# Down projection of a decoder block's FFN: nine of its 22 pairs of channel tiles as two-by-two block products with seven multiplications instead of eight

## The chip, the cores and the metric

One core of a Trainium2 chip runs the whole kernel. The metric is the device time of one execution in microseconds (us), the median over the runs shown; lower is better.

## The reference

A decoder block: RWKV-7 time mixing and a forgetting attention run side by side over 272 positions (16 meta tokens and 256 tokens), are gated and merged, pass `w_o`, and are added to the residual `h`. Then comes the feed-forward part, which is where the change lies. All is float32.

```python
gate, up = jnp.split(_rms(h, n2) @ w_gu, 2, axis=-1)
return h + (jax.nn.silu(gate) * up) @ w_dn
```

Here `w_gu` is 2048 x 11264 and `w_dn` 5632 x 2048; the last product, the down projection, takes the activation `a` = silu(gate) * up, 256 tokens x 5632 channels, to 256 x 2048.

## The kernel before, in words

**Products in three parts.** A float32 operand is split in two fp32r parts, a high one (a copy, made by ScalarE) and a low one (operand minus high, made by VectorE). A product is three matmuls into the same PSUM bank: high by high, low by high, high by low. Each weight tile of 128 x 1024 numbers (512 KB) is loaded by a DMA issued on SyncE into a buffer `raw` (four of them, `RAWB`), then split into `wh` (ScalarE, L324) and `wl` (VectorE, L325), of which there are four each (`WB`). All this is in `wload`.

**Jobs.** The work is a list of jobs. A job has a `load` (the DMA and the split) and a `mul` (the matmuls); `run` calls the load of a job and then the `mul` of the one before, so that loads are written one job ahead. Only TensorE keeps the order in which it is written (`manual_schedule`). For ScalarE, VectorE, GpSimd and SyncE the framework's scheduler lays the instructions of the whole program into one fixed row per engine, by data that it expects to be ready and free buffers; on the chip each engine takes its row strictly in order and waits on semaphores. `slot` counts the time of the matmuls written so far and lets generators that were handed to `spawn` write their next step when it is due.

**Gate and up.** Eleven blocks of 512 channels; `post_up` (L1382 to L1388) multiplies, and `split`s the activation into `ach` and `acl` (128 channels x 44 channel tiles x 256 tokens, high and low). `ga` is a group of eight buffers of 128 x 256 for the gates, `ub` two such buffers.

**Down projection (L1391 to L1403).** Four blocks `j` of 512 output columns. In each, `tm_jobs` (L1297) runs over 22 pairs of channel tiles: a job loads two tiles of 128 channels x 512 columns and makes 12 matmuls: two channel tiles by two token tiles by three parts. `dn` is the accumulator, one PSUM bank for each token tile. The activation is the stationary operand (128 x 128), the weight the moving one (512 columns). After pair 22, `post` adds the bank to the residual in `hh` on VectorE (L1400) and writes it out; the last block does so in halves, one of them on ScalarE's queue.

PSUM has eight banks: four `main` (used by `dn`) and four `aux`.

The few lines of the loop on TensorE:

```python
for k, t in ((0, 0), (1, 0), (0, 1), (1, 1)):
    ...
    nc.tensor.matmul(o, ah[:, kt, ts_], hi, start=first, stop=False)
    nc.tensor.matmul(o, al[:, kt, ts_], hi, start=False, stop=False)
    nc.tensor.matmul(o, ah[:, kt, ts_], lo_, start=False, stop=last)
```

## Time and profile before

| | us |
|---|---|
| median of 3 runs | 1526.89 (1526.59 to 1528.88) |
| the profiled execution's own time | 1526.46 |
| its span, first to last instruction | 1524.8 |
| down projection on TensorE, first to last matmul | 1278.0 to 1520.6 |

The granted TensorE clock is 1.00 over the run. Times inside the execution count from the start of the span. In the profile PE is TensorE's matmuls, PEld its weight loads, DVE VectorE, ACT ScalarE, POOL GpSimd, SP SyncE. The columns of a group are busy us and mean ns of one instruction, then the idle time ahead of it on its engine and what ended it.

### The profile page before, as it was taken

Reading aid. Unit: us, or ns where it says so; the run is one execution under the profiler, and the core shown is the slowest. Engines: PE = TensorE matmul, PEld = TensorE weight load, DVE = VectorE, ACT = ScalarE, POOL = GpSimd, SP = SyncE. Lnnn points to the kernel's source line nnn. Section 1 sums busy time; section 2 is a strip of 40 time slices with the busy share of each in tenths; the row PEclk is TensorE's granted clock in tenths of the full one; section 3 lists DMA queues with packets and bytes.
Section 4 is the critical chain, followed back from the end, with each engine's and each line's share of the span. In section 5 each row is a group of like instructions: output and inputs, shape, how many; then the busy total and the mean of one; then the engine's idle time right before and its main releaser. Section 6 shows DMA issues by size and latency. Waiting matters only on the chain.

```text
span 1524.8 us, 25932 instructions
## 1 busy us (share of the span) xinstructions
PE 1518.6 (100%) x10113; PEld 1347.6 (88%) x10113; DVE 1028.4 (67%) x1853; ACT 781.1 (51%) x1184; POOL 103.1 (7%) x182
## 2 busy tenths in 40 slices
PE   9999999999999999999999999999999999999999
PEld 9999999989989888998888888888888888888887
DVE  8888699699689758776565566656556665444443
ACT  7754665564475545554455455545545554333332
POOL 2121203302202100000000000000000000000000
PEclk9999999999999999999999999999999999999999
DMA  8567456646645847767566666666666666666663
GB/s 273 164 178 200 130 143 187 179 116 178 187 125 156 224 143 224 234 221 246 181 180 182 192 192 186 192 190 192 186 191 191 190 191 188 191 205 205 191 204 105
DMA packets 211931, 283.30 MB, mean 186 GB/s; under 512 B 24096, under 2 KB 129072, under 8 KB 211808
## 3 DMA queue, kind: packets, MB, share of 16 engines
q1 hardware_dynamic: 206912, 277.25, 61.9%
q10 hardware_dynamic: 4896, 4.40, 0.8%
q8 instruction: 79, 1.29, 0.3%
q14 instruction: 44, 0.36, 0.1%
HBM read 274.36 MB, written 7.24 MB: 185 GB/s over the span
## 4 chain that ended last, share of the span: by engine, by line
PE 98%; ACT 1%; DVE 0%; DMA 0%; issue 0%; SPq 0%; DVEq 0%; ACTq 0%
PE up L430 11%; PE gt L430 10%; PE zg L430 8%; PE dn L1317 5%; PE dn L1319 5%; PE dn L1318 5%; PE up L432 5%; PE gt L432 5%; PE zg L432 4%; PE f L354 2%; PE f L356 2%; PE f L355 2%; PE br L354 2%; PE br L355 2%; PE br L356 2%; PE wo L1317 2%
## 5 line engine op out<-in xcount | busy, mean ns | idle before, releaser
L325 DVE TENSOR_TENSOR wl<-raw,wh 128x1024 fp32r<-128x1024 f32 x488 | 597.8, 1226 | 409.5 <-ACT wh L324 406.5
L324 ACT ACTIVATE wh<-raw 128x1024 fp32r<-128x1024 f32 x488 | 516.8, 1060 | 597.9 <-PE dn L1318 140.0
L430 PE MATMUL gt<-hts,wh 128*128 128x512 f32 x704 | 242.9, 392 | 0.0
L430 PE MATMUL up<-hts,wh 128*128 128x512 f32 x704 | 242.7, 392 | 0.0
L432 PE MATMUL gt<-hts,wl 128*128 128x256 f32 x660 | 184.8, 280 | 0.0
L432 PE MATMUL up<-hts,wl 128*128 128x256 f32 x660 | 184.5, 280 | 0.0
L430 PE MATMUL zg<-xhl,wh 128*128 128x512 f32 x512 | 181.2, 399 | 0.0
L430 PEld LDWEIGHTS up<-hts,wh 128*128 128x128 f32 x704 | 129.9, 188 | 25.2
L430 PEld LDWEIGHTS gt<-hts,wh 128*128 128x128 f32 x704 | 129.9, 188 | 25.1
L1317 PE MATMUL dn<-wh,ach 128*128 128x512 f32 x352 | 138.3, 393 | 0.0
L1319 PE MATMUL dn<-wl,ach 128*128 128x512 f32 x352 | 138.1, 392 | 0.0
L1318 PE MATMUL dn<-wh,acl 128*128 128x512 f32 x352 | 137.7, 391 | 0.0
L432 PE MATMUL zg<-xhl,wl 128*128 128x256 f32 x480 | 134.3, 280 | 0.0
L432 PEld LDWEIGHTS up<-hts,wl 128*128 128x128 f32 x660 | 125.3, 190 | 1.8
L432 PEld LDWEIGHTS gt<-hts,wl 128*128 128x128 f32 x660 | 125.3, 190 | 1.8
L430 PEld LDWEIGHTS zg<-xhl,wh 128*128 128x128 f32 x512 | 94.3, 188 | 18.7 <-issue 0.7
L432 PEld LDWEIGHTS zg<-xhl,wl 128*128 128x128 f32 x480 | 91.0, 190 | 1.2
L1319 PEld LDWEIGHTS dn<-wl,ach 128*128 128x128 f32 x352 | 66.0, 187 | 15.3
L1318 PEld LDWEIGHTS dn<-wh,acl 128*128 128x128 f32 x352 | 66.1, 188 | 14.9
L1317 PEld LDWEIGHTS dn<-wh,ach 128*128 128x128 f32 x352 | 66.1, 188 | 14.6
L354 PE MATMUL f<-xhl,wh 128*128 128x272 f32 x256 | 76.3, 298 | 0.0
L356 PE MATMUL f<-xhl,wl 128*128 128x272 f32 x256 | 73.7, 288 | 0.0
(463 smaller groups left out, 2789.6 us busy)
## 6 DMA issues: line engine op xcount, KB each, us to landing
raw<-in_w_gate_up_dram SPq DMA_DIRECT2D x176, 512.0 KB, 4.3
raw<-in_w_in_dram SPq DMA_DIRECT2D x160, 512.0 KB, 3.8
raw<-in_w_down_dram SPq DMA_DIRECT2D x88, 512.0 KB, 4.6
raw<-in_w_o_dram SPq DMA_DIRECT2D x32, 512.0 KB, 3.9
raw<-in_w_branch_a_dram SPq DMA_DIRECT2D x16, 512.0 KB, 4.4
raw<-in_w_branch_b_dram SPq DMA_DIRECT2D x16, 512.0 KB, 3.8
zgd<-zg ACTq DMA_DIRECT2D x30, 128.0 KB, 3.8
gate<-zgd SPq DMA_DIRECT2D x15, 256.0 KB, 5.5
```

The lines of the kernel that those rows point to most:

```text
L324: nc.scalar.activation(th, rr, AF.Copy)
L325: nc.vector.tensor_tensor(tl, rr, th.bitcast(F32), op=ALU.subtract)
L354: nc.tensor.matmul(ps, wh, ah, start=first, stop=False)
L355: nc.tensor.matmul(ps, wh, al, start=False, stop=False)
L356: nc.tensor.matmul(ps, wl, ah, start=False, stop=last)
L430: nc.tensor.matmul(ps.rearrange("p (a t) -> p a t", a=2), wh, act, start=first, stop=last)
L432: nc.tensor.matmul(ps[:, :T], wl, act[:, 0, :], start=False, stop=False)
L1317: nc.tensor.matmul(o, ah[:, kt, ts_], hi, start=first, stop=False)
L1318: nc.tensor.matmul(o, al[:, kt, ts_], hi, start=False, stop=False)
L1319: nc.tensor.matmul(o, ah[:, kt, ts_], lo_, start=False, stop=last)
```

## The change

**Layout.** The output columns are taken in two halves of 1024 (`cg`), not in four blocks. For a pair of channel tiles and a half, the weight is a block matrix of two channel tiles by two column blocks, b11, b12, b21, b22, and the activation one of two token tiles by two channel tiles, a11, a12, a21, a22. Four accumulators `cs` (`dn00` to `dn03`: c11, c12, c21, c22) take the four `main` banks.

**Slow pairs** (13 of 22) are as before: eight products of three matmuls, in two jobs of one column block each (`slow_jobs`).

**Fast pairs** (4 to 12, `FAST`) use seven products (`fast_jobs`), in the Winograd form of Strassen's scheme. With S1 = a21+a22, S2 = S1-a11, S3 = a11-a21, S4 = a12-S2 and T1 = b12-b11, T2 = b22-T1, T3 = b22-b12, T4 = b21-T2, the products are: a11 b11, S1 T1, S2 T2, S3 T3, each into a bank of its own (`dnp`: the four `aux` banks, summed over all fast pairs); S4 b22 into c12, a12 b21 into c11, a22 T4 into c21. After the last fast pair of a half, `sums_of_products` (L1546 to L1548) adds the four banks into the residual `hh`: one ScalarE copy and eight VectorE additions of 128 x 512.

**Loads of a fast pair.** Two `raw` buffers (`ra`: b11, b12; `rb`: b22, b21), filled by one DMA of 512 KB and two of 256 KB. Four jobs: b11 is split (half a tile), then b22 and b21, then T1 to T4 are made by four VectorE subtractions of 128 x 512 (L1510) into two buffers `tt`, and split as two tiles.

**Sums of the activation** (`sums_of_pairs`). S1 to S4 for all nine fast pairs are made once, in five batches (two pairs each, the last one): ten GpSimd operations of 128 x 256 (L1427; 128 x 128 in the last) into four `ga` buffers, then four ScalarE copies (L1440) and four VectorE subtractions (L1441) split them into `sst` (S1 to S3), and S4 into the place of a21 in `ach`/`acl`. The batches' buffers are `s2`, `s4`, `s6`, `s8`, `s9` with the number of the sum behind (`s60` is the first of the third batch). The third batch takes over the buffers of the first, the fourth those of the second, the second those of the last gates (`ga100` to `ga103`).

**Order.** First half: slow pairs 0 to 3, then nine times a fast and a slow pair. Second half: slow pair 0, nine times a fast and a slow pair, three slow pairs.

On each engine the program's rows stand as follows; numbers behind names tell buffers apart. First ScalarE at the start of the down projection, before. `wh_14431`, `wh_14449`, `wh_14467` are the weights of jobs 3, 4 and 5 (counted from 0).

```order
L324 ACTIVATE wh_14431<-raw_14430 128x4x256
L436 ACTIVATE ub102_14360<-up10_2_14174 128x256
L436 ACTIVATE ub103_14367<-up10_3_14175 128x256
L324 ACTIVATE wh_14449<-raw_14448 128x4x256
L499 ACTIVATE ach_9874<-ub102_14360 128x256
L499 ACTIVATE ach_9874<-ub103_14367 128x256
L324 ACTIVATE wh_14467<-raw_14466 128x4x256
L324 ACTIVATE wh_14485<-raw_14484 128x4x256
L324 ACTIVATE wh_14503<-raw_14502 128x4x256
L324 ACTIVATE wh_14521<-raw_14520 128x4x256
```

The same place after; `wh_14488` and `wh_14506` are jobs 5 and 6.

```order
L1440 ACTIVATE sst_14324<-s42_14448 128x2x128
L1440 ACTIVATE ach_9874<-s43_14449 128x2x128
L332 ACTIVATE wh_14488<-raw_14487 128x4x256
L507 ACTIVATE ach_9874<-ub102_14375 128x256
L507 ACTIVATE ach_9874<-ub103_14382 128x256
L1440 ACTIVATE sst_14324<-s60_14525 128x2x128
L1440 ACTIVATE sst_14324<-s61_14526 128x2x128
L1440 ACTIVATE ach_9874<-s63_14528 128x2x128
L1440 ACTIVATE sst_14324<-s62_14527 128x2x128
L332 ACTIVATE wh_14506<-raw_14505 128x4x256
L332 ACTIVATE wh_14546<-raw_14545 128x4x256
```

Between the weight copies now stand the copies of the sums: job 5's copy stands behind all four copies of the second batch, and job 6's behind all four of the third; each of these waits for GpSimd.

Next VectorE a little later, before: the last split of the activation, and splits of weights.

```order
L500 TENSOR_TENSOR acl_9875<-ub102_14360,ach_9874 128x256
L500 TENSOR_TENSOR acl_9875<-ub103_14367,ach_9874 128x256
L325 TENSOR_TENSOR wl_14468<-raw_14466,wh_14467 128x4x256
L325 TENSOR_TENSOR wl_14486<-raw_14484,wh_14485 128x4x256
L325 TENSOR_TENSOR wl_14504<-raw_14502,wh_14503 128x4x256
```

The same engine after, at the first fast pair. `wl_14596` and `wl_14598` are the splits of T1, T2 and of T3, T4; `raw_14673` and `raw_14674` are `ra` and `rb` of the next fast pair.

```order
L508 TENSOR_TENSOR wl_14585<-raw_14564,wh_14584 128x4x256
L1441 TENSOR_TENSOR sst_14324<-s81_14622,sst_14324 128x2x128
L1441 TENSOR_TENSOR sst_14324<-s82_14623,sst_14324 128x2x128
L1441 TENSOR_TENSOR acl_9875<-s83_14624,ach_9874 128x2x128
L1441 TENSOR_TENSOR sst_14324<-s90_14709,sst_14324 128x128
L1441 TENSOR_TENSOR sst_14324<-s91_14710,sst_14324 128x128
L508 TENSOR_TENSOR wl_14596<-tt_14599,wh_14595 128x4x256
L1441 TENSOR_TENSOR sst_14324<-s92_14711,sst_14324 128x128
L1510 TENSOR_TENSOR tt_14727<-raw_14673 128x512
L1441 TENSOR_TENSOR acl_9875<-s93_14712,ach_9874 128x128
L1510 TENSOR_TENSOR tt_14727<-raw_14674,tt_14727 128x512
L508 TENSOR_TENSOR wl_14598<-tt_14600,wh_14597 128x4x256
```

The splits of the fourth and fifth batch's sums (L1441) stand ahead of both weight splits of the first fast pair, and the next pair's first subtraction (from `raw_14673`) stands ahead of the current pair's last split. The second of these repeats: T1 of the next pair stands ahead of the last split in eight of the first half's fast pairs, and in four later pairs of the second half.

Last VectorE where one block of columns ends and the next begins, before.

```order
L325 TENSOR_TENSOR wl_14756<-raw_14754,wh_14755 128x4x256
L325 TENSOR_TENSOR wl_14778<-raw_14776,wh_14777 128x4x256
L325 TENSOR_TENSOR wl_14798<-raw_14796,wh_14797 128x4x256
L1400 TENSOR_TENSOR hh_9122<-dn0_0_14380,hh_9122 128x512
L1400 TENSOR_TENSOR hh_9122<-dn0_1_14381,hh_9122 128x512
L325 TENSOR_TENSOR wl_14816<-raw_14814,wh_14815 128x4x256
```

The same engine after, where the first half ends: `wl_15322` is the last split of pair 12, `wl_15347` and `wl_15369` the two jobs of the last slow pair, `wl_15391` the first job of the second half.

```order
L508 TENSOR_TENSOR wl_15322<-tt_15324,wh_15321 128x4x256
L333 TENSOR_TENSOR wl_15347<-raw_15345,wh_15346 128x4x256
L1548 TENSOR_TENSOR hh_9122<-dnp00_14588,hh_9122 128x512
L1548 TENSOR_TENSOR u0_15357<-dnp02_14590,u0_15357 128x512
L1548 TENSOR_TENSOR hh_9122<-dnp01_14589,hh_9122 128x512 x2
L1548 TENSOR_TENSOR hh_9122<-u0_15357,hh_9122 128x512
L333 TENSOR_TENSOR wl_15369<-raw_15367,wh_15368 128x4x256
L1548 TENSOR_TENSOR u0_15357<-dnp03_14591,u0_15357 128x512
L1556 TENSOR_TENSOR hh_9122<-dn00_14395,hh_9122 128x512
L1548 TENSOR_TENSOR hh_9122<-u0_15357,hh_9122 128x512 x2
L1556 TENSOR_TENSOR hh_9122<-dn02_14397,hh_9122 128x512
L333 TENSOR_TENSOR wl_15391<-raw_15389,wh_15390 128x4x256
```

The additions of the products' banks (L1548) and of the accumulators (L1556) stand between the splits of the jobs that TensorE takes next.

The diff, without its blank lines (of the functions above all is shown):

```diff
--- before.py
+++ after.py
@@ -63,6 +63,14 @@
 LANES = 108
 BETWEEN = 2
 MIX = 0.47
+FAST = [4, 5, 6, 7, 8, 9, 10, 11, 12]
+BATCHES = (2, 2, 2, 2, 1)
+SLOW = [0, 1, 2, 3] + list(range(13, 22))
+ORDER = [SLOW[:4] + [i for pair in zip(FAST, SLOW[4:]) for i in pair],
+         SLOW[:1] + [i for pair in zip(FAST, SLOW[1:10]) for i in pair] + SLOW[10:]]
+PAIRS = 8000
 HOP = 3050
 PREP = 5200
@@ -1388,18 +1396,174 @@
                 split(ach[:, 4 * j + m, :], acl[:, 4 * j + m, :], ub)
         run(cm_jobs(wgu[:, j * 512:(j + 1) * 512], KT, hts, NMETA, T, post_gate, name=f"gt{j}"))
         run(cm_jobs(wgu[:, DFF + j * 512:DFF + (j + 1) * 512], KT, hts, NMETA, T, post_up, alloc=aux_ps, name=f"up{j}"))
     wdn = A["w_down"][0]
-    for j in range(4):
-        js = slice(j * 512, (j + 1) * 512)
-        def post(t, ps, j=j):
-            n = 256 if j == 3 else 512
-            for c in range(512 // n):
-                cs_ = slice(j * 512 + c * n, j * 512 + (c + 1) * n)
-                nc.vector.tensor_tensor(hh[:, t, cs_], ps[:, c * n:(c + 1) * n], hh[:, t, cs_], op=ALU.add)
-                (nc.scalar if c else nc.sync).dma_start(out[0][t * P:(t + 1) * P, cs_], hh[:, t, cs_])
-        run(tm_jobs(wdn[:, js], NF, ach, acl, post, f"dn{j}"))
+    fast = FAST
+    slow = [i for i in range(NF // 2) if i not in fast]
+    acp_h, acp_l = (t.rearrange("p (i k) (t c) -> p i k t c", k=2, t=2) for t in (ach, acl))
+    sst = hp.tile([P, KT, 2, L], F32R, tag="hts", name="sst").rearrange("p k a t -> p (k a t)")
+    sst = sst[:, :len(fast) * 6 * P].rearrange("p (i s a c) -> p i s a c", i=len(fast), s=3, a=2)
+    def sums_of_pairs():
+        at = 0
+        for n in BATCHES:
+            fs, ps_ = slice(at, at + n), slice(fast[at], fast[at] + n)
+            at += n
+            h = lambda k, t: acp_h[:, ps_, k, t, :].bitcast(F32)
+            l = lambda k, t: acp_l[:, ps_, k, t, :].bitcast(F32)
+            f = [sst[:, fs, i, 1, :] for i in range(3)] + [acp_l[:, ps_, 0, 1, :]]
+            hi = [sst[:, fs, i, 0, :] for i in range(3)] + [acp_h[:, ps_, 0, 1, :]]
+            f32 = [hp.tile([P, T], F32, tag="ga", name=f"s{at}{i}", bufs=8)[:, :n * P].rearrange("p (i c) -> p i c", c=P)
+                   for i in range(4)]
+            def tt(i, x_, y_, op):
+                nc.gpsimd.tensor_tensor(f32[i], x_, y_, op=op)
+            tt(0, h(0, 1), h(1, 1), ALU.add)
+            tt(0, f32[0], l(0, 1), ALU.add)
+            tt(0, f32[0], l(1, 1), ALU.add)
+            tt(1, f32[0], h(0, 0), ALU.subtract)
+            tt(1, f32[1], l(0, 0), ALU.subtract)
+            tt(2, h(0, 0), h(0, 1), ALU.subtract)
+            tt(2, f32[2], l(0, 0), ALU.add)
+            tt(2, f32[2], l(0, 1), ALU.subtract)
+            tt(3, h(1, 0), f32[1], ALU.subtract)
+            tt(3, f32[3], l(1, 0), ALU.add)
+            yield PAIRS
+            for i in range(4):
+                nc.scalar.activation(hi[i], f32[i], AF.Copy)
+                nc.vector.tensor_tensor(f[i], f32[i], hi[i].bitcast(F32), op=ALU.subtract)
+    def a_of(i, k, t):
+        return acp_h[:, i, k, t, :], acp_l[:, i, k, t, :]
+    def s_of(i, n):
+        return a_of(i, 0, 1) if n == 3 else tuple(sst[:, fast.index(i), n, a, :] for a in range(2))
+    def rows(ap):
+        return ap.rearrange("p (r c) -> p r c", c=T)
+    def product(ps, a, w, half, first, last):
+        o = ps.rearrange("p (a c) -> p a c", a=2)
+        hi, lo_ = (x_[:, 2 * half:2 * half + 2] for x_ in w)
+        nc.tensor.matmul(o, a[0], hi, start=first, stop=False)
+        nc.tensor.matmul(o, a[1], hi, start=False, stop=False)
+        nc.tensor.matmul(o, a[0], lo_, start=False, stop=last)
+        slot(3 * 512 / 2.4)
+    def split_tiles():
+        return [wp.tile([P, WCOLS], F32R, tag=t, name=t, bufs=WB).rearrange("p (r c) -> p r c", c=L)[:, :, s:s + T]
+                for t, s in zip(("wh", "wl"), PLACE_T)]
+    def slow_jobs(i, cg, cs, end):
+        def mk(x_):
+            def load():
+                j = 2 * cg + x_
+                return wload([(P, 0, [2, 512], [((ALL,), kblock(wdn[i * 256:(i + 1) * 256, j * 512:(j + 1) * 512]))])],
+                             1024, lay=(None, *PLACE_T))
+            def mul(w):
+                if not cs:
+                    cs.extend(main_ps(f"dn{cg}{n}") for n in range(4))
+                first = i == slow[0]
+                for t in range(2):
+                    for k in range(2):
+                        product(cs[2 * t + x_], a_of(i, k, t), w[0], k, first and k == 0, end and k == 1)
+                    if end:
+                        post(cg, t, x_, cs[2 * t + x_])
+            return load, mul
+        return [mk(0), mk(1)]
+    def fast_jobs(i, cg, cs, ps, end):
+        box = {}
+        def b(k, x_):
+            return wdn[i * 256 + k * P:i * 256 + (k + 1) * P, cg * 1024 + x_ * 512:cg * 1024 + (x_ + 1) * 512]
+        def load0():
+            ra, rb = (wp.tile([P, 1024], F32, tag="raw", name="raw", bufs=RAWB) for _ in range(2))
+            nc.sync.dma_start(ra, wdn[i * 256:i * 256 + P, cg * 1024:(cg + 1) * 1024])
+            for x_ in range(2):
+                nc.sync.dma_start(rb[:, (1 - x_) * 512:(2 - x_) * 512], b(1, x_))
+            box["r"] = rows(ra), rows(rb)
+            w = split_tiles()
+            split(*(t[:, 0:2] for t in w), box["r"][0][:, 0:2])
+            return w
+        def load1():
+            w = split_tiles()
+            split(*w, box["r"][1])
+            return w
+        def load2():
+            (b11, b12), (b22, b21) = ([r[:, 0:2], r[:, 2:4]] for r in box["r"])
+            w, v = split_tiles(), split_tiles()
+            ts = [rows(hp.tile([P, 1024], F32, tag="tt", name="tt", bufs=2)) for _ in range(2)]
+            t1, t2, t3, t4 = (t[:, 2 * n:2 * n + 2] for t in ts for n in range(2))
+            for o, x_, y_ in ((t1, b12, b11), (t2, b22, t1), (t3, b22, b12), (t4, b21, t2)):
+                nc.vector.tensor_tensor(o, x_, y_, op=ALU.subtract)
+            split(*w, ts[0])
+            box["v"] = v, ts[1]
+            return w
+        def load3():
+            v, t = box["v"]
+            split(*v, t)
+            return v
+        first = i == fast[0]
+        def mul0(w):
+            if not ps:
+                ps.extend(aux_ps(f"dnp{cg}{n}") for n in range(4))
+            product(ps[0], a_of(i, 0, 0), w, 0, first, end)
+        def mul1(w):
+            product(cs[1], s_of(i, 3), w, 0, False, False)
+            product(cs[0], a_of(i, 1, 0), w, 1, False, False)
+        def mul2(w):
+            product(ps[1], s_of(i, 0), w, 0, first, end)
+            product(ps[2], s_of(i, 1), w, 1, first, end)
+        def mul3(w):
+            product(ps[3], s_of(i, 2), w, 0, first, end)
+            product(cs[2], a_of(i, 1, 1), w, 1, False, False)
+            if end:
+                sums_of_products(cg, ps)
+        return [(load0, mul0), (load1, mul1), (load2, mul2), (load3, mul3)]
+    def sums_of_products(cg, ps):
+        p1, p5, p6, p7 = ps
+        h11, h12, h21, h22 = (hh[:, t, (2 * cg + x_) * 512:(2 * cg + x_ + 1) * 512] for t in range(2) for x_ in range(2))
+        u = hp.tile([P, 512], F32, tag="jk", name=f"u{cg}", bufs=2)
+        nc.scalar.activation(u, p1, AF.Copy)
+        for o, x_ in ((u, p6), (h11, p1), (h12, p5), (h12, u), (u, p7), (h22, p5), (h21, u), (h22, u)):
+            nc.vector.tensor_tensor(o, x_, o, op=ALU.add)
+    def post(cg, t, x_, ps):
+        j = 2 * cg + x_
+        n = 256 if j == 3 else 512
+        for c in range(512 // n):
+            cs_ = slice(j * 512 + c * n, j * 512 + (c + 1) * n)
+            nc.vector.tensor_tensor(hh[:, t, cs_], ps[:, c * n:(c + 1) * n], hh[:, t, cs_], op=ALU.add)
+            (nc.scalar if c else nc.sync).dma_start(out[0][t * P:(t + 1) * P, cs_], hh[:, t, cs_])
+    spawn(sums_of_pairs(), 0)
+    for cg in range(2):
+        cs, ps = [], []
+        for i in ORDER[cg]:
+            if i in fast:
+                run(fast_jobs(i, cg, cs, ps, i == fast[-1]))
+            else:
+                run(slow_jobs(i, cg, cs, i == ORDER[cg][-1]))
     finish_job()
     hp_pool.__exit__(None, None, None)
     ap_pool.__exit__(None, None, None)
```

## Prediction

> **What bounds the kernel now.** I read the page first: its span, its busy shares, and the chain that ended last.
>
> ```profile
> span 1524.8 us, 25932 instructions
> PE 1518.6 (100%) x10113; PEld 1347.6 (88%) x10113; DVE 1028.4 (67%) x1853; ACT 781.1 (51%) x1184; POOL 103.1 (7%) x182
> PE 98%; ACT 1%; DVE 0%; DMA 0%; issue 0%; SPq 0%; DVEq 0%; ACTq 0%
> ```
>
> TensorE (PE) is busy to 100% and makes 98% of the chain: a matmul taken out is time saved, and any wait that a change puts in front of a matmul is time lost. Then the stage itself, by 50 us stretches (columns: PE, PEld, DVE, ACT, POOL busy, clock, DMA share), and the accumulator's instructions with who waits for them.
>
> ```profile
> 1300.00:1350.00 50.00, 50.00 (x219) 40.76 (x219) 23.34 (x20) 19.43 (x19) 0.00 (x0) 1.00 0.64 202
> ...
> L1317 PE MATMUL dn<-wh,ach x352: 392/394/399, 1278.0 to 1520.2; 128*128 128x512 f32 x176
> ...
> L1319 PE MATMUL dn<-wl,ach x352: 392/392/393, 1278.4 to 1520.6; 128*128 128x512 f32 x176
> ...
>   ACT wh L324: 140.0, 84
> ```
>
> In the stage PE never idles; VectorE (DVE) is busy under half, ScalarE (ACT) 39%, GpSimd (POOL) not at all. ACT waits for PE to free weight buffers: the feeders run ahead of PE by as many buffers as there are. 1056 matmuls start between 1278.0 and 1520.6: 242.6 / 1055 = 0.230 us each, so a job of 12 is 2.76 us and a slow pair 5.52.
>
> **What the change removes.** 9 pairs x 2 halves x 3 = 54 matmuls: 54 x 0.230 = **-12.4 us**, in full, if the others stay back to back. A fast pair's 21 take 4.83 us, fast and slow together 10.35.
>
> **What it adds, and where.** Prices of the feeders, from the groups, the buffer `raw` and the timeline of DVE:
>
> ```profile
> L1400 DVE TENSOR_TENSOR hh<-dn,hh 128x512 f32<-128x512 f32 x6 | 4.1, 688 | 0.2
> ...
> L324 ACT ACTIVATE wh<-raw x84: 1062/1062/1065, 1280.7 to 1509.8; 128x1024 fp32r<-128x1024 f32 x84
> ...
> DMA to landing us min/median/max: 3.8/4.5/5.0
> ...
> 1273.57 1.23 DVE L325 TENSOR_TENSOR wl<-raw,wh 128x1024 fp32r<-128x1024 f32 x1 [1.55 <-ACT wh L324]
> ...
> 1278.83 0.75 DVE L1387 TENSOR_TENSOR ub<-ub,ga 128x256 f32<-128x256 f32 x2
> 1279.50 1.21 DVE L325 TENSOR_TENSOR wl<-raw,wh 128x1024 fp32r<-128x1024 f32 x1
> 1280.63 0.75 DVE L500 TENSOR_TENSOR acl<-ub,ach 128x256 fp32r<-128x256 f32 x2
> ...
> 1284.32 0.75 DVE L1387 TENSOR_TENSOR ub<-ub,ga 128x256 f32<-128x256 f32 x2
> ...
> 1338.13 1.45 DVE L1400 TENSOR_TENSOR hh<-dn,hh 128x512 f32<-128x512 f32 x2
> ```
>
> Back to back, a split of 128 x 1024 takes DVE 1.13 us (1279.50 to 1280.63), one of 128 x 256 0.33 (two from 1278.83 to 1279.50), and by the line through both 0.60 for 128 x 512; an addition out of PSUM 0.69 to 0.76. A fast pair then costs DVE 0.60 + 3 x 1.13 + 4 x 0.60 = 6.4, a slow one 2.3: 8.7 of PE's 10.35. The sums fit; what decides is who waits for whom in each engine's row.
>
> *Alternation of pairs.* DVE's row has the next pair's first subtraction ahead of the current pair's last split, so DVE stands still until the next `ra` has landed, with that split and two slow ones queued behind it. The buffer comes free only with the third subtraction. From landing to that point DVE has 4 x 0.60 + 3 x 1.13 + 0.1 = 5.9 us; then the DMA. Loop: 5.9 + 4.5 = 10.4, against 10.35. With the row's 3.8 it hides, with 5.0 it costs 0.55 a pair: 0 to 6 us over eleven such pairs; I take **+1.5**, by the median. The waits on buffers close inside that loop. SyncE's extra issue per fast pair has idle time to lie in.
>
> *Turn of the halves.* Behind the last split of pair 12 DVE has a split (1.1), five additions (0.6 to 0.72 each, 3.5), then the split that PE needs 0.92 + 2.76 + 0.46 = 4.1 us after that last split (four matmuls, a job, two matmuls on the high part): ready at 5.75, 1.6 late. Then five more additions (4.1, to 9.1, with the accumulators' first two) and a split, to 10.25, needed at 5.75 + 2.3 + 0.46 = 8.5: 1.75 late, and 0.3 follows. At the second half's end the 1.6 comes again. In all 5.2; if DVE is a microsecond ahead at both, 3.2. Taken: **+4.2**.
>
> *Opening of the stage.* This is the largest term. Prices of GpSimd, by groups; then DVE alone and POOL alone in one stretch where both work:
>
> ```profile
> L485 POOL TENSOR_TENSOR zd<-z 128x256 f32<-128x256 f32 x8 | 4.9, 612 | 25.7 <-DVE z L480 25.6
> L1115 POOL TENSOR_SCALAR b<-bias,cq,hs 128x144 f32<-128x144 f32 x16 | 9.4, 594 | 44.6 <-DMA bias<-ncd 44.6
> L1118 POOL TENSOR_TENSOR bias<-bias,cmask 128x256 f32<-128x256 f32 x8 | 5.9, 737 | 0.0
> ...
> 242.01 1.21 DVE L325 TENSOR_TENSOR wl<-raw,wh 128x1024 fp32r<-128x1024 f32 x1
> 243.15 0.75 DVE L888 TENSOR_TENSOR lt<-lx,ln 108x52 f32<-108x52 f32 x1
> 243.93 0.67 DVE L890 TENSOR_TENSOR lx<-lx,lt 108x52 f32<-108x52 f32 x1
> 244.63 0.24 DVE L888 TENSOR_TENSOR lt<-lx,ln 108x75 f32<-108x75 f32 x1
> ...
> 242.00 1.83 POOL L1117 TENSOR_TENSOR b<-b,cmask 128x256 f32<-128x256 f32 x1
> 243.78 0.74 POOL L1118 TENSOR_TENSOR bias<-bias,cmask 128x256 f32<-128x256 f32 x1
> ```
>
> Alone, a GpSimd operation of 128 x 256 takes 0.61 to 0.74 (0.69 taken; half of it, 0.35, for half the width is an estimate; the row of about that width, another operation with collisions in it, has 0.59, which would add 2 us at most). In the collision, POOL's 1.83 is DVE's split of 1.21 and then its own 0.6; DVE's next two small ones take 0.75 and 0.67 where 0.24 is usual for more columns: the engines take turns.
>
> Count from T, PE's first matmul of the stage (1278.0). Job 6 (slow pair 3) is needed at T + 6 x 2.76 = 16.5, its low part at 17.0. Its ACT copy stands behind the third batch's copies, so behind 30 GpSimd operations. The first batch is done before T. Five of the second start when the first two gate buffers are read (T + 1.5); the other five wait for the last gate (1284.32 + 0.75: T + 7.1); ten more follow. Without collisions: 7.1 + 15 x 0.69 = 17.5, then ACT's copy of the last sum and of the weight (0.4 + 1.06) and the split (1.2): T + 20.1, 3.1 late. From there to the last split of the first fast pair DVE has four splits of 1.13, seven operations of 0.60 (six subtractions, two of them the next pair's, and the half split), and 16 splits of sums (12 of 0.33, four of half the width, 0.22): 13.6 us. PE has work for 9.0 (ten matmuls left of job 6, job 7, 15 matmuls of the fast pair and two before the low part): 4.6 late. Sum: **8 us**. With turns taken at each meeting: five GpSimd operations push the last gate back by some 1.6, and DVE's two weight splits and three small ones that meet the next fifteen cost 2 x 1.13 + 3 x 0.33 = 3.2 (the third batch ends at T + 22.3, job 6's split 7.9 late); in the later stretch ten operations of 0.6 and ten of 0.35 come between DVE's: 13.6 + 9.5 = 23.1 against 9.0, 14.1 late. Sum: **22 us**. A gain here is excluded, since PE cannot take a job before its matmuls are through. Each meeting in the quoted stretch was a collision, so I take **+18**, near the upper end, less what falls into waits of DVE.
>
> By the Trainium skill ("SBUF — State Buffer", section "SBUF: two separate sides") VectorE and GpSimd share a pair of SBUF ports under an exclusive lock: a VectorE operation with two SBUF inputs and a GpSimd operation that reads SBUF never run together, and the loser waits for the whole instruction. The trace agrees (1.83 = 1.21 + 0.6). By that rule alone the opening would be the 22, without it the 8.
>
> *At nothing.* The first batch's GpSimd work lies under the last gate block, where DVE idles 1.55 us of each 2.77; without that cover, ten turns of 0.6. ACT's 5.8 us in 10.35 and the four DMAs that write the first half out lie under PE. The end of the program is as before.
>
> **Sum.** -12.4 + 18 + 1.5 + 4.2 = +11.3. The profiled execution took 1526.46 (span 1524.8 and 1.66 around it), 0.4 under the median 1526.89, so the sum goes onto the median: **1538.2 us**. With its own uncertainties this case spans 1532 to 1544.
>
> **Rivals.**
> *The opening hides* (0.20). If GpSimd's operations of the second and third batch took about 0.3 us each, or began that much earlier, the third batch would end at 7.1 + 15 x 0.3 = T + 11.6, job 6's split at 14.2, 2.8 early, and of DVE's 4.6 some 2 would be left: -12.4 + 2 + 1.5 + 4.2 = -4.7: 1522.2. For it: a row laid out by the scheduler supposes that these sums are ready there. Against: no operation of that width and two inputs in the trace is under 0.61. It decides at T + 13: a third batch that ends earlier leaves a gain of over 3 us.
> *No collisions* (0.13). The opening costs 8: +1.3, 1528.2, no change that can be told. For it: DVE often waits for GpSimd there, and while it waits it holds nothing. Against: the 1.83 us.
> *DMA sets the pace as well* (0.12). Landing at 5.0 after each release (+6), the opening at 22, the turns at 5.2: -12.4 + 33.2 = +20.8, 1547.7. For it: landings near 5.0 are in the row; against: that row has the larger traffic of a transfer each 2.76 us.
> The forecast has 0.55.
>
> **Range and chances.** 1520 to 1548 holds the forecast and the second rival, most of the first and half of the third. A run of this kernel can tell 0.2% (3 us) from no change: faster 0.20 (the first rival), same 0.12 (the second, mostly), slower 0.68.
>
> **What would show it.** Right: 352 x 3 - 54 = 1002 matmuls of the stage; PE idle some 18 us between T + 11 and T + 50, with ACT's copies of weights released by POOL sums and DVE's splits of sums waiting for POOL; POOL's L1427 at about 1.2 us or more instead of 0.69; two short gaps of PE behind pair 12 of the first half; DVE's first subtraction released by the DMA of `raw`. Wrong: PE without gaps in the first 50 us of the stage (first rival); L1427 near 0.7 and DVE's splits at 1.2 (second); gaps of 0.5 us in each fast pair (third).

## The result, and the profile after

| | us |
|---|---|
| before, median of 4 runs | 1526.84 (1526.59 to 1528.88) |
| after, median of 4 runs | 1541.35 (1540.28 to 1543.03) |
| after over before | 1.0096, interval 1.0083 to 1.0108 |
| the profiled execution after, its span | 1540.52, 1538.8 |

The change makes the kernel 14.5 us slower; 11.3 were forecast. The page of the changed kernel: span, busy shares, chain that ended last.

```profile
span 1538.8 us, 26254 instructions
PE 1515.8 (99%) x10059; PEld 1337.7 (87%) x10059; DVE 1133.0 (74%) x1997; ACT 816.1 (53%) x1242; POOL 148.1 (10%) x232
PE 90%; DVE 3%; DMA 2%; POOL 2%; issue 1%; ACT 1%; SPq 0%; DVEq 0%; POOLq 0%; ACTq 0%
```

The 54 matmuls are gone (10113 to 10059), and 8 points of the chain went from PE to the feeders. Where, the start of the stage in stretches of 10 us tells (PE, PEld, DVE, ACT, POOL busy, then the clock).

```profile
1280.00:1290.00 10.00, 9.99 (x44) 7.82 (x42) 10.00 (x13) 6.48 (x15) 9.45 (x11) 1.00 0.29 96
1290.00:1300.00 10.00, 6.90 (x26) 4.75 (x27) 6.60 (x8) 3.15 (x5) 6.79 (x8) 1.00 0.33 107
1300.00:1310.00 10.00, 5.19 (x22) 3.60 (x21) 7.05 (x8) 1.94 (x5) 9.31 (x10) 1.00 0.33 105
1310.00:1320.00 10.00, 5.07 (x11) 2.64 (x11) 8.37 (x14) 3.95 (x8) 6.16 (x10) 0.53 0.31 105
...
1330.00:1340.00 10.00, 10.00 (x46) 8.12 (x44) 8.00 (x10) 5.83 (x6) 0.00 (x0) 1.00 0.62 202
```

From 1280 to 1290 GpSimd works and VectorE has no gap, and TensorE is still full. From 1290 to 1320 TensorE is starved; in the last line shown, with POOL at zero, it is full again. Next the waits of the stage (who for whom; us in total, times, longest), and what PE waited for at job 4, at jobs 6 and 7 (slow pair 3) and at the first fast pair.

```profile
DVE tt L1510 <- DMA raw<-in_w_down_dram: 23.3, 11, 2.6
ACT sst L1440 <- POOL s L1427: 17.9, 10, 3.5
ACT ach L1440 <- POOL s L1427: 5.3, 3, 3.7
```

```profile
1291.39 0.50 PE L1457 MATMUL dn<-wl,ach 128*128 128x512 f32 x1 [1.40 <-DVE wl L333]
...
1298.19 0.50 PE L1455 MATMUL dn<-wh,ach 128*128 128x512 f32 x1 [0.78 <-ACT wh L332]
...
1304.69 0.50 PE L1457 MATMUL dn<-wl,ach 128*128 128x512 f32 x1 [2.19 <-DVE wl L333]
...
1309.89 0.51 PE L1455 MATMUL dnp<-wh,ach 128*128 128x512 f32 x1 [2.62 <-ACT wh L507]
...
1315.07 0.80 PE L1457 MATMUL dn<-wl,ach 128*128 128x512 f32 x1 [2.70 <-DVE wl L508]
...
1319.38 0.80 PE L1455 MATMUL dnp<-wh,sst 128*128 128x512 f32 x1 [2.24 <-ACT wh L507]
...
1330.31 0.39 PE L1455 MATMUL dnp<-wh,ach 128*128 128x512 f32 x1
```

ScalarE's copies of sums wait for POOL, ScalarE's copies of weights stand behind those, and PE waits for them and for the splits that follow. The first loss is another one: the splits of jobs 4 and 5 came late out of VectorE's full row (1291.39), which cost 2.3 us before PE waited for any copy of ScalarE.

How losses are counted, here and below: a matmul that waits for nothing starts 0.2304 us after the one before. The 96 of the four slow pairs then take 22.1 us, a fast and a slow pair (45) 10.37. What lies between the starts of two fast pairs' first matmuls beyond that is lost. The stage starts at 1278.32; the first fast pair starts at 1309.89, 31.6 later, so 9.5 lost; the second at 1330.31, 20.4 later, 10.1 lost. The later loops of the first half lost 3.0; the turn of the halves, from the first half's last fast pair to the end of the second half's first one, 1.0; the loops behind it 2.1. Together 25.7; the whole stage is 256.3 long, which is 1001 x 0.2304 = 230.6 and 25.7.

### The profile page after: what moved, and what is told of

It reads as the page before. It is cut to its first block, busy times and chain, and to the rows that moved or that the text cites. A ratio compares the mean times of both kernels' runs of the same rounds, so it can differ in the third digit from the quotient of the medians.

```text
span 1538.8 us, 26254 instructions
## 1 busy us (share of the span) xinstructions
PE 1515.8 (99%) x10059; PEld 1337.7 (87%) x10059; DVE 1133.0 (74%) x1997; ACT 816.1 (53%) x1242; POOL 148.1 (10%) x232
## 4 chain that ended last, share of the span: by engine, by line
PE 90%; DVE 3%; DMA 2%; POOL 2%; issue 1%; ACT 1%; SPq 0%; DVEq 0%; POOLq 0%; ACTq 0%
PE up L438 10%; PE gt L438 10%; PE zg L438 8%; PE up L440 5%; PE gt L440 5%; PE zg L440 4%; PE f L362 2%; PE dn L1455 2%; PE dn L1456 2%; PE dn L1457 2%; PE f L364 2%; PE f L363 2%; DMA raw<-in_w_down_dram 2%; PE br L362 2%; PE br L363 2%; PE br L364 2%
## 5 line engine op out<-in xcount | busy, mean ns | idle before, releaser
L333 DVE TENSOR_TENSOR wl<-raw,wh 128x1024 fp32r<-128x1024 f32 x452 | 557.9, 1239 | 286.9 <-ACT wh L332 286.1
L332 ACT ACTIVATE wh<-raw 128x1024 fp32r<-128x1024 f32 x452 | 477.6, 1059 | 465.1 <-PE up L438 120.1
L1457 PE MATMUL dn<-wl,ach 128*128 128x512 f32 x262 | 103.7, 397 | 7.2 <-DVE wl L333 4.5
L1455 PE MATMUL dn<-wh,ach 128*128 128x512 f32 x262 | 103.7, 396 | 0.8 <-ACT wh L332 0.8
L1456 PE MATMUL dn<-wh,acl 128*128 128x512 f32 x262 | 103.2, 394 | 0.0
L1427 POOL TENSOR_TENSOR s<-ach 128x256 f32<-128x256 f32 (+1 forms) x10 | 9.5, 947 | 719.8 <-DVE ub L1395 704.8
L362 PE MATMUL f<-xhl,wh 128*128 128x272 f32 x256 | 76.3, 298 | 0.0
L363 PE MATMUL f<-xhl,wh 128*128 128x272 f32 x256 | 73.6, 288 | 0.0
L507 ACT ACTIVATE wh<-tt 128x1024 fp32r<-128x1024 f32 x36 | 37.8, 1059 | 58.9 <-PE dn L1456 44.5
```

Of the source, the lines that this page charges most:

```text
L332: nc.scalar.activation(th, rr, AF.Copy)
L333: nc.vector.tensor_tensor(tl, rr, th.bitcast(F32), op=ALU.subtract)
L362: nc.tensor.matmul(ps, wh, ah, start=first, stop=False)
L363: nc.tensor.matmul(ps, wh, al, start=False, stop=False)
L507: nc.scalar.activation(hi, src, AF.Copy)
L1427: nc.gpsimd.tensor_tensor(f32[i], x_, y_, op=op)
```

## The experiments

All kernels were timed beside the kernel before on the same chip (its medians there: 1526.5 to 1526.8). Losses in us from the profiled execution of each.

| kernel | median us | over before (interval) | before 1st fast pair | 1st loop | other loops of 1st half | turn | rest | all |
|---|---|---|---|---|---|---|---|---|
| after | 1541.35 | 1.0096 (1.0083 to 1.0108) | 9.5 | 10.1 | 3.0 | 1.0 | 2.1 | 25.7 |
| no sums (left out) | 1525.62 | 0.9993 (0.9984 to 1.0002) | 0 | 0.2 | 5.6 | 1.0 | 4.1 | 11.0 |
| one `tt` buffer | 1535.91 | 1.0060 (1.0045 to 1.0075) | 9.5 | 9.9 | 0 | 1.0 | 0 | 20.5 |
| written order | 1536.75 | 1.0064 (1.0048 to 1.0081) | 8.8 | 6.5 | 0.7 | 4.9 | 0.9 | 21.9 |
| sums on VectorE | 1528.48 | 1.0013 (1.0003 to 1.0022) | 0 | 0.1 | 9.5 | 1.0 | 3.5 | 14.2 |
| VectorE, one `tt` | 1523.58 | 0.9982 (0.9973 to 0.9990) | 0 | 0.1 | 7.4 | 1.0 | 0.3 | 8.8 |
| the same, six slow pairs first | 1522.07 | 0.9970 (0.9959 to 0.9982) | 0 | 2.6 | 0.4 | 3.0 | 0.6 | 6.6 |
| no sums (left out), one `tt` | 1516.18 | 0.9933 (0.9918 to 0.9948) | 0 | 0 | 0 | 1.0 | 0.1 | 1.1 |
| VectorE, one `tt`, paced | 1517.07 | 0.9938 (0.9924 to 0.9951) | 0 | 0 | 0.8 | 1.3 | 0.7 | 2.8 |
| GpSimd, one `tt`, paced | 1534.82 | 1.0052 (1.0035 to 1.0069) | 7.3 | 11.6 | 0 | 1.0 | 0.2 | 20.2 |
| written after two pairs | 1532.24 | 1.0040 (1.0026 to 1.0054) | 3.7 | 8.1 | 0 | 5.1 | 0.9 | 17.7 |
| the same, paced | 1529.82 | 1.0021 (1.0011 to 1.0031) | 0 | 3.2 | 6.5 | 4.2 | 0.9 | 14.8 |

The theory after the result: the opening is lost because ScalarE's and VectorE's rows wait for GpSimd's sums, which the meetings with VectorE make slow; the alternation is lost because VectorE's row waits for the next pair's rows. The rivals: the loss is of the fast pairs themselves (VectorE's work, the transfers), or of the row order alone.

**Without GpSimd's sums.**

```diff
-            f32 = [hp.tile([P, T], F32, tag="ga", ...) for i in range(4)]
-            tt(0, h(0, 1), h(1, 1), ALU.add)
...
+            f32 = [h(0, 0), h(1, 1), h(1, 0), h(1, 1)]
```

> The ten GpSimd sums of each batch are left out: ScalarE and VectorE split parts of the activation itself in their place, as many and as wide as before, so the products of the fast pairs are not those of the reference. Theory (the opening's loss is engines' rows that wait for GpSimd, and turns taken with it): job 6 is split in time, VectorE's 13.6 us fit into its slack, the opening costs 0 to 1 instead of 19.6; with 5.6 for the alternation and 1.2 for the turns -12.4 + 0.5 + 6.8 = -5.1, about 1522. Rival (VectorE's own added work is the bound, GpSimd only stands beside it): the opening keeps over 10 of its 19.6, above 1531.

Measured 1525.62. The opening's loss went from 19.6 to 0.2, so all of it hangs on those sums. The time stayed above the 1522 expected, because the alternation lost more than in the changed kernel: VectorE's waits for the DMA of `raw` grew.

```profile
DVE tt L1496 <- DMA raw<-in_w_down_dram: 30.2, 13, 3.1
```

**One buffer for T1 to T4.** One buffer of 2048 columns in place of two of 1024: the next pair's T1 can then not be written before the present pair's last split has read it, so the scheduler cannot put it ahead.

```diff
-            ts = [rows(hp.tile([P, 1024], F32, tag="tt", name="tt", bufs=2)) for _ in range(2)]
+            tb = hp.tile([P, 2048], F32, tag="tt", name="tt", bufs=1)
+            ts = [rows(tb[:, n * 1024:(n + 1) * 1024]) for n in range(2)]
```

> T1 to T4 in one buffer of 2048 columns instead of two of 1024, so that the next pair's first subtraction can't stand ahead of the current pair's last split. Theory (VectorE stands still at that subtraction until the next ra has landed): no wait of a subtraction for a DMA, the alternation's 5.6 falls under 1, about 1536.5. Rival (the loop over landing and release binds anyway, at rb or at the split of b11): the wait moves to another instruction, 1540 to 1542.

Measured 1535.91, and every loop of the alternation at 10.37 or 10.38. First VectorE's row in the changed kernel, with the issue of that pair's `ra`; then VectorE with one buffer.

```profile
1369.53 0.34 SPq L1491 DMA_DIRECT2D raw<-in_w_down_dram  x1
...
1371.13 1.22 DVE L508 TENSOR_TENSOR wl<-tt,wh 128x1024 fp32r<-128x1024 f32 x1
1374.83 0.69 DVE L1510 TENSOR_TENSOR tt<-raw 128x512 f32<-128x512 f32 x1 [2.49 <-DMA raw<-in_w_down_dram]
1375.44 1.22 DVE L508 TENSOR_TENSOR wl<-tt,wh 128x1024 fp32r<-128x1024 f32 x1
```

```profile
1359.56 1.41 DVE L1511 TENSOR_TENSOR tt<-raw,tt 128x512 f32<-128x512 f32 x2
1361.45 1.22 DVE L508 TENSOR_TENSOR wl<-tt,wh 128x1024 fp32r<-128x1024 f32 x1 [0.48 <-ACT wh L507]
1363.58 1.23 DVE L508 TENSOR_TENSOR wl<-tt,wh 128x1024 fp32r<-128x1024 f32 x1 [0.90 <-ACT wh L507]
1364.72 2.36 DVE L333 TENSOR_TENSOR wl<-raw,wh 128x1024 fp32r<-128x1024 f32 x2
```

In the first, T1 stands between the two splits and waits 2.49 us for a transfer; in the second the splits follow each other, and no wait for the DMA is left.

**The written order.** ScalarE's and VectorE's rows of the whole stage as the code writes them.

```diff
+    with tc.manual_schedule(engines={nc.scalar.engine, nc.vector.engine}):
-    spawn(sums_of_pairs(), 0)
-    for cg in range(2):
+        spawn(sums_of_pairs(), 0)
+        for cg in range(2):
...
```

> ScalarE and VectorE take the down projection's instructions in the order in which they are written, nothing else changed: each batch's copies and splits stand 8 us of matmuls behind its sums, and no subtraction of a next pair is taken forward. Theory: the opening keeps only what the turns with GpSimd cost VectorE, 5 to 8 us, the alternation under 1, the turns rise to about 4 since all eight additions stand together: -12.4 + 6.5 + 0.5 + 4 = -1.4, about 1525.5 (1523 to 1531). Rival (VectorE's work and its collisions are what binds, not the rows): 1535 or more, since the work is the same.

Measured 1536.75: missed by 11 us, and by the number the rival's. One wait explains 7 of them: the last activation block's chains now stand ahead of the first weight copies, and PE waits at the stage's start.

```profile
PE dn L1455 <- ACT wh L332: 6.7, 1, 6.7
```

The other 8.6 of the opening stayed, and the turn rose to 4.9. So the row order is not the whole of it; the run below mends the start.

**The sums on VectorE.**

```diff
-                nc.gpsimd.tensor_tensor(f32[i], x_, y_, op=op)
+                nc.vector.tensor_tensor(f32[i], x_, y_, op=op)
```

> The sums of the activation on VectorE instead of GpSimd, the same operations. Theory: no turns and no waits between engines, but 50 operations of 0.33 (0.2 for half the width) more on VectorE; counting its row, the first fast pair comes about 1 us late and the second about 6.6 more: opening 7 to 8 instead of 19.6, about 1529 (1526 to 1533). Rival (VectorE's own work is the bound): 15 us more of it make the time longer than 1541, about 1548 or more.

Measured 1528.48. The opening's loss is 7.4 (within the second fast pair) instead of 19.6, though VectorE has 50 operations more to do.

**Both undone.** The sums on VectorE and one buffer for T1 to T4 together.

> Both single undoings together: the sums of the activation's blocks stand on VectorE instead of GpSimd, and T1 to T4 of a pair share one buffer, so that VectorE's row can no longer hold the next pair's T1 ahead of the present pair's last split. If the two losses are apart (the opening through GpSimd's sums, the alternation through VectorE's wait for the next pair's rows), they add: 1528.5 with the sums on VectorE, less its 6.2 of the alternation, plus the 0.4 that was left of it with one buffer, so 1522.7 (1521 to 1525), with about 7 lost at the second fast pair as before and every alternation within 0.1. Rival, that the wait for the rows comes from how far ahead VectorE is and moves elsewhere when its row is changed: 1528 or more, with the lost time at other products.

Measured 1523.58, faster than before: the two losses are apart and add. What is left is 7.3 in the second fast pair.

**Six slow pairs first.** As above, with the first half as six slow pairs, then fast and slow in turn, with two fast neighbours twice.

```diff
-ORDER = [SLOW[:4] + [i for pair in zip(FAST, SLOW[4:]) for i in pair],
+ORDER = [SLOW[:6] + [i for pair in zip(FAST, SLOW[6:11]) for i in pair] + FAST[5:7] + SLOW[11:12] + FAST[7:] + SLOW[12:],
```

> As the kernel with the sums on VectorE and one buffer, and with six slow pairs instead of four ahead of the first fast pair of the first half (further on in that half two places then have two fast pairs one behind the other). If the 7 us that are lost at the second fast pair are VectorE's work on the sums that has too few slow pairs to hide in, two more slow pairs (11 us of TensorE, 2.45 us each of VectorE's splits, so 6.1 us of cover) take all but about 1 of it away, and the two neighbouring fast pairs cost 0 to 2: 1517 to 1520. Rival, that the row order puts the sums ahead of the splits however many slow pairs stand before them, so the loss stays at the same place of VectorE's row: 1522 or more.

Measured 1522.07. By time this is at the edge of the rival's range, but the loss did not stay: of 7.3 lost in the second fast pair's loop 0 was left there, and 2.6, not 1, were lost in the first one's, since the later batches' sums still stand ahead of the first fast pair's splits, and the turn, just behind the two neighbours, lost 3.0 instead of 1.0.

**No sums, one buffer.** The first two edits together.

> Leaves the sums of the activation's blocks out (parts of the activation stand in their place as operands), so that GpSimd does nothing in the stage, and lets T1 to T4 share one buffer. Neither of the two losses has its cause then. If they are all there is, the 54 matmuls show in full less the turn of the halves: 1526.8 - 12.4 + 0.3 (opening) + 0.5 (alternation) + 1.1 (turn) = 1516.3 (1515 to 1518). Rival, that TensorE is held by something else once those are gone (the transfers, ScalarE's copies): 1520 or more, with losses of over 0.2 at products that had none so far.

Measured 1516.18. With both causes gone the loss is 1.1 in the whole stage: the matmuls taken out show nearly in full, and neither the transfers nor the fast pairs' splits hold TensorE.

**The sums beside the kernel before.** 50 GpSimd sums of the same size and number, read by nobody, where the kernel before does the end of its up blocks and the start of the down projection.

```diff
+                    slot(3 * 512 / 2.4)
...
+    def sums_alone():
+        for n, at in ((2, 4), (2, 6), (2, 8), (2, 10), (1, 12)):
+            f = hp.tile([P, T], F32, tag="ga", ...)
+            for m in range(5):
+                for k in range(2):
+                    nc.gpsimd.tensor_tensor(f, acp_h[:, at:at + n, k, 0, :]..., acp_l[:, at:at + n, k, 1, :]..., op=ALU.add)
+            yield 8000
+    spawn(sums_alone(), 0)
```

> The kernel before with the same 45 sums on GpSimd added at the start of the down projection, from the same operands and with nobody who reads them: the meeting of GpSimd and VectorE alone, without the sums' splits and without fast pairs. If two-operand operations of the two engines hold each other up, GpSimd's 128x256 sums take 0.9 us and more in the mean instead of 0.6 to 0.7, and single splits of VectorE go from 1.22 to 1.7 us; the time stays at 1526.8 (to 1528), since VectorE's splits of 2.45 us per 5.5 us of TensorE leave it more than half idle there. Rival, that they do not hold each other up and the long durations in the changed kernel were waits for operands: splits at 1.22 and sums at 0.6 to 0.7 here. Second rival, that the meeting alone holds TensorE up: 1530 or more.

(The expectation says 45; there are 50.) Measured 1526.45, ratio 1.0000 (0.9991 to 1.0009). Over the 80 us from 1235 to 1315, in which the sums run, first this kernel's sum and one stretch of its VectorE, then the kernel before's:

```profile
sum 80.00, PE 80.00 PEld 68.14 DVE 64.59 ACT 38.36 POOL 53.35; mean PE 20.00 PEld 17.03 DVE 16.15 ACT 9.59 POOL 13.34
...
1248.01 8.48 DVE L325 TENSOR_TENSOR wl<-raw,wh 128x1024 fp32r<-128x1024 f32 x5
```

```profile
sum 80.00, PE 80.00 PEld 68.09 DVE 46.71 ACT 37.96 POOL 0.00; mean PE 20.00 PEld 17.02 DVE 11.68 ACT 9.49 POOL 0.00
...
1248.65 1.23 DVE L325 TENSOR_TENSOR wl<-raw,wh 128x1024 fp32r<-128x1024 f32 x1 [1.59 <-ACT wh L324]
```

VectorE does the same work and is busy 17.9 us longer, 0.36 us for each of the 50 sums; five splits that took 1.23 each come back to back at 1.70. A sum takes 1.07 us in the mean (53.35 / 50, ten of them of half the width) instead of the 0.6 to 0.7 of the full width. TensorE doesn't feel it, since VectorE had idle time there: the meeting costs nothing by itself, and its price is VectorE's room.

**Paced.** As with the sums on VectorE and one buffer, and the batches of sums twice as far apart.

```diff
-PAIRS = 8000
+PAIRS = 16000
```

> The sums on VectorE, T1 to T4 in one buffer, four slow pairs first as in the changed kernel, and the batches of sums 16 us of the plan apart instead of 8. VectorE's sums and their splits are about 14 operations of 0.34 us a batch, 22 us in all; a slow pair leaves it 5.5 - 2.45 = 3.1 us and a fast and a slow pair 10.35 - 8.35 = 2.0 us. With 8 us between batches all of it stands in the row by the second fast pair, where only 4 x 3.1 + 2.0 = 14.4 us of room had been: 8 us too much, and 7.3 were lost there. With 16 us two batches and the sums of the third are due by then (13 us), and the rest where the next pairs leave room. If that account holds, the loss at the second fast pair falls to 0 to 1.5 and no other place has over 1: 1526.5 - 12.4 + 1 (opening) + 0.9 (alternation) + 1.4 (turn) = 1517.4 (1515.5 to 1519.5). Rival, that the loss only spreads over the later fast pairs because VectorE has no room there: 1521 to 1524.

Measured 1517.07 (1516.56 to 1518.24): 9.6 us faster than the kernel before, the fastest of the versions that leave nothing out. The second and third fast pair's first matmuls without the pacing, then with it:

```profile
1310.58 0.39 PE L1455 MATMUL dnp<-wh,ach 128*128 128x512 f32 x1
...
1328.22 0.40 PE L1455 MATMUL dnp<-wh,ach 128*128 128x512 f32 x1
```

```profile
1310.61 0.39 PE L1455 MATMUL dnp<-wh,ach 128*128 128x512 f32 x1
...
1320.98 0.39 PE L1455 MATMUL dnp<-wh,ach 128*128 128x512 f32 x1
```

17.6 us apart before, 10.37 now, with the same instructions.

**Paced, on GpSimd.** One buffer and the distance of 16 us, the sums where the change has them.

> The changed kernel with one buffer for T1 to T4 and with the batches of sums 16 us of the plan apart instead of 8, the sums still on GpSimd and the rows laid by the scheduler. The scheduler still puts the splits of all five batches' sums ahead of the first fast pair's last two weight splits, since nothing that its rows suppose holds GpSimd back. If the opening's loss is that row and GpSimd's slow sums, spreading them in the plan alone changes nothing: 18 to 20 lost up to the second fast pair, 1536 (1534 to 1537.5), as with one buffer alone (1535.9). Rival, that the distance between the batches is what made the gain with the sums on VectorE, whatever the row: 10 lost or less, 1527 or under.

Measured 1534.82, with 18.9 lost up to the second fast pair. GpSimd's row is not held back by the plan: its sums end at 1317, in the changed kernel at 1318. VectorE's row still has all splits of sums ahead of the first fast pair's last split (two of the fifth batch's four stand between the pair's last two weight splits, in the changed kernel too; the others ahead of both). In the scheduler's rows the pacing helped only where VectorE does the sums.

**Written order after two pairs, and the same paced.**

```diff
     spawn(sums_of_pairs(), 0)
+    cs = []
+    for i in ORDER[0][:2]:
+        run(slow_jobs(i, 0, cs, False))
+    with tc.manual_schedule(engines={nc.scalar.engine, nc.vector.engine}):
...
```

> The changed kernel (sums on GpSimd, two buffers for T1 to T4), with ScalarE's and VectorE's instructions kept in the order in which they are written from the third slow pair on. In the first run with the written order from the stage's start, 7 us were lost right at its start, since the last up block's copies and chains then stood where they are written; with the first two slow pairs left to the scheduler these should be gone, and the rest of that run should stay: 1536.8 - 7 = 1529.7 (1528 to 1531.5), with 6 to 10 lost up to the second fast pair instead of 19.6. That much of the opening's loss would then be the row in which the third to fifth batches' splits stand far too early, and the rest VectorE's work slowed by GpSimd. Rival, that the row is not what matters, since GpSimd's 46 us of sums hold VectorE up wherever their splits stand: 1536 or more.

> As the run with the written order from the third slow pair on, and with the batches of sums 16 us of the plan apart instead of 8: VectorE meets GpSimd's sums over some 80 us instead of 45, and the splits of the sums are spread as far. If VectorE's lack of room in the opening is what is left there, 3 (0 to 6) are lost up to the third fast pair instead of 6 to 10, and the time is 1524 (1521 to 1527). Rival, that a sum on GpSimd costs VectorE about what it takes wherever it runs, and the pairs behind the opening have no room for it: as without the spread, 1528 to 1531.

Measured 1532.24 and 1529.82, 2.5 and 6 above what was expected. The artefact at the start is gone, and the row order is worth 7.8 of the opening's 19.6 (11.8 are left). The pacing takes away what was lost ahead of the first fast pair (3.7) and spreads the rest over the first five loops of a fast and a slow pair (3.2, 2.4, 1.2, 2.1, 0.7): 9.7 instead of 11.8. Up to the third fast pair 5.6 were lost, within what was expected, but 4 more behind it, and the time is the rival's. Why it stays above the run with VectorE's own sums is seen in VectorE's busy time, 84 us from the stage's start (sums of seven stretches of 12 us); first GpSimd's sums in the written order and paced, then VectorE's own sums, paced, with one stretch each:

```profile
1314.00:1326.00 12.00, 10.43 (x43) 7.62 (x42) 12.00 (x9) 5.60 (x6) 11.77 (x10) 1.00 0.46 145
...
sum 84.00, PE 77.18 PEld 59.75 DVE 82.88 ACT 42.58 POOL 47.57; mean PE 11.03 PEld 8.54 DVE 11.84 ACT 6.08 POOL 6.80
```

```profile
1314.00:1326.00 12.00, 12.00 (x53) 9.76 (x53) 11.96 (x18) 6.68 (x8) 0.00 (x0) 1.00 0.59 185
...
sum 84.00, PE 84.00 PEld 68.07 DVE 83.13 ACT 48.54 POOL 0.00; mean PE 12.00 PEld 9.72 DVE 11.88 ACT 6.93 POOL 0.00
```

VectorE is busy nearly all the time in both, the time that it is held up included. Over the seven stretches the counts of its operations add up to 100 with GpSimd working beside it and to 148 without, 37 sums among the 148: beside GpSimd it got less of its other work done, too. (The two runs also differ in the buffer for T1 to T4 and in the row order.)

## Why the prediction was right, point by point

**The matmuls: right.** 54 fewer, and with the losses' causes gone (no sums, one buffer) the kernel is 10.3 us faster with 1.1 lost. The profiled executions, to which the losses belong, are 11.2 apart (1524.8 and 1513.6), so 12.3 of the 12.4 are found.

**The opening, +18: right, 19.6, with one wait left out.** GpSimd's operations beside VectorE (line of the sums, ns min/median/max), the end of the third batch, job 6's split, and VectorE from there to the first fast pair's last split, with the busy time of that stretch:

```profile
L1427 POOL TENSOR_TENSOR s<-s,acl x30: 498/801/1719, 1236.2 to 1317.5; 128x256 f32<-128x256 f32 x24, 128x128 f32<-128x128 f32 x6
...
1293.65 3.09 POOL L1427 TENSOR_TENSOR s<-s,acl 128x256 f32<-128x256 f32 x3
...
1298.17 1.22 DVE L333 TENSOR_TENSOR wl<-raw,wh 128x1024 fp32r<-128x1024 f32 x1 [3.40 <-ACT wh L332]
...
1302.90 1.74 DVE L333 TENSOR_TENSOR wl<-raw,wh 128x1024 fp32r<-128x1024 f32 x1
...
1309.87 0.69 DVE L508 TENSOR_TENSOR wl<-raw,wh 128x512 fp32r<-128x512 f32 x1 [2.95 <-ACT wh L507]
...
1322.11 1.21 DVE L508 TENSOR_TENSOR wl<-tt,wh 128x1024 fp32r<-128x1024 f32 x1
...
1299.39:1323.32 23.93, 14.09 (x39) 8.56 (x39) 19.35 (x29) 8.70 (x15) 15.60 (x20) 0.73 0.27 88
```

The third batch ends at 1296.74, T + 18.4 (forecast T + 17.5 without meetings, 22.3 with them). Job 6's split ends at 1299.39, T + 21.1 (20.1 to 24.9), 4.1 late. The first fast pair's last split ends at 1323.32, 23.9 later (13.6 to 23.1), where PE had work for 9.0. So the first step came out near its lower end and the second above its upper end. VectorE's operations in the second step are those that were counted, 13.6 us by the forecast's prices, and it was busy for 19.35: the meetings added 5.7 there, not 9.5 (at 1302.90 a split takes 1.74 instead of 1.22). For the other 4.6 it stood idle for ScalarE's copies of weights (2.95 at 1309.87, 1.63 at 1319.36), which stand behind the copies of the fourth and fifth batch's sums; the forecast had such a wait only for job 6. Meetings that cost less and a wait that was left out made up for each other, so that 18 came this near to 19.6 is in part luck.

The forecast that L1427 takes 1.2 us or more is off: 0.80 in the median of these, both widths together, and 0.90 in the mean of all 50 (148.1 - 103.1 us of POOL in the two pages). By its own sign (0.7 or 1.2) this lies nearer to the rival without collisions; the lengthened splits tell against that rival. While VectorE waited, from 1306.9 to 1309.8, sums of the full width took 0.70 to 0.72.

That the meetings cost VectorE time is shown by more runs: GpSimd's sums lengthen VectorE's work by 0.36 us each beside the kernel before, and VectorE's whole busy time is 1133.0 us with the sums on GpSimd and this with them on VectorE, one buffer and pacing:

```profile
PE 1508.0 (99%) x10059; PEld 1336.7 (88%) x10059; DVE 1131.5 (75%) x2047; ACT 813.6 (54%) x1242; POOL 101.5 (7%) x182
```

50 more operations in the same busy time: handing them to GpSimd took nothing off VectorE. The Trainium skill says so too ("Perfetto Trace Analysis", section "Optimizing Scalar/DVE Operations"): since the two share a port, moving operations between them might not help. The runs agree. The prediction did not weigh that the sums would be cheaper on VectorE itself.

**The alternation, +1.5: right in mechanism, too small, 5.1.** The term that was mis-sized is the 4.5 us in "Loop: 5.9 + 4.5 = 10.4". `ra` was issued at 1369.53 and T1 began at 1374.83: 5.3, not 4.5. In six such loops it took 5.0, 4.2, 4.4, 5.3, 5.3 and 5.4, and in three of the second half 4.4, 5.1 and 5.4; with 5.96 from T1 to the next issue (1363.57 to 1369.53) the loop is 10.2 to 11.4, and where it is above 10.37 PE loses about the difference. The row of these transfers' landings looks as before:

```profile
DMA to landing us min/median/max: 3.8/4.3/5.0
```

But such a row holds only the landings that the profile has: 4 of these 18 transfers, and 22 of the stage's 81 in the row that the prediction used. Where there is one and T1 waits for it, T1 starts 0.1 us later (landed at 1363.47, T1 at 1363.57), so nearly all of the 5.3 is the transfer. The row's 3.8 to 5.0 was too low a range for these loops: six of the nine lie at 5.0 or more. Why these transfers take longer stays open. One buffer removes the loss whole, which settles the cause.

**The turn of the halves, +4.2: wrong, 1.0.** Two steps failed. The first is the start of the count, "behind the last split of pair 12": it supposed VectorE just in time there. Pair 12 is the first half's last fast pair, so no T1 of a next pair stands in its row, and the wait of 1.4 to 2.6 us in each pair before it falls away (VectorE's last two splits, and PE's first matmul on the second of them):

```profile
1405.07 1.22 DVE L508 TENSOR_TENSOR wl<-tt,wh 128x1024 fp32r<-128x1024 f32 x1
1407.05 1.23 DVE L508 TENSOR_TENSOR wl<-tt,wh 128x1024 fp32r<-128x1024 f32 x1 [0.77 <-ACT wh L507]
...
1409.86 0.39 PE L1457 MATMUL dnp<-wl,sst 128*128 128x512 f32 x1
```

No T1 stands between the two, and the last split ends at 1408.28, 1.6 us before PE takes it. At the end of the second half the lead is 1.6 too (1510.25 and 1511.84). That takes 3.2 off the 5.2 that were counted. The second step that failed is "two matmuls on the high part" ahead of the low part of the next half's first job:

```profile
1416.54 0.40 PE L1456 MATMUL dn<-wh,acl 128*128 128x512 f32 x1
1416.78 0.40 PE L1455 MATMUL dnp<-wh,ach 128*128 128x512 f32 x1
...
1417.73 0.50 PE L1457 MATMUL dn<-wl,ach 128*128 128x512 f32 x1
...
1424.78 0.50 PE L1455 MATMUL dnp<-wh,sst 128*128 128x512 f32 x1 [0.55 <-ACT wh L507]
```

Four matmuls stand between the second on the high part (1416.54) and the first on the low part (1417.73), two of them of the second half's first fast pair (`dnp`). So TensorE does not keep the written order everywhere, other than the section on the kernel before says: by the starts in the trace the order differs in this stage at 34 of 1002 places, all between 1416 and 1430. The low part was needed 0.9 later than counted, and the split, done at 1417.67, was just in time. 5.2 - 3.2 - 0.9 = 1.1 is the size of what was lost, but not in the two gaps that were forecast: nearly all of it stands at the second half's first fast pair (1424.78), whose copy came late. (The prediction's "five more additions (4.1, to 9.1)" does not add up: from 5.75 to 9.1 is 3.4. Its later figures go by the 9.1.) In the runs with written order, whose rows are others, the turn cost 4.2 to 5.1 and the end 0.8.

**The sum: right by two errors that cancel, which is luck.** -12.4 + 19.6 + 5.1 + 1.0 = +13.3, against 14.0 between the spans (of the rest 0.3 is the stage's later start, 0.4 the pace of 0.2304 against 242.6 / 1055 = 0.2300 before). The alternation was 3.6 too small and the turn 3.2 too large. Of the rivals, "the opening hides" and "no collisions" are refuted by the opening's loss. Of "DMA sets the pace as well" the +6 for the alternation was nearer than the forecast's 1.5; that the transfers set the pace whatever the row is refuted by the run with one buffer, whose transfers are of the same sizes and whose loops lose nothing.

Left open: why the scheduler's rows place the sums' splits where they do, and how much of the opening with GpSimd is the meetings alone, since the runs without them change the rows as well.

## What to carry to other kernels

Work handed from a busy VectorE to GpSimd was not free here: price it by VectorE's own time beside it (here 0.36 us for each sum) before calling the other engine idle. A step that removes TensorE work gains only as much as the feeders have room at that place; the same instructions cost 7.3 us or nothing, depending on how far apart the batches stand. Look in an engine's row for an instruction of the next step that waits for a transfer ahead of the present step's last one; tying its buffer to that last one moves it back.
